# The decoder trunk's up-projections: four more chunks by seven products, a product moved behind the next chunk's first one, and work moved from VectorE to GpSimd

## The chip, the cores and the metric

One Trainium2 chip, one core of it. The core has five engines, each with an instruction queue of its own: TensorE (PE; its weight loads are listed as PEld), VectorE (DVE), ScalarE (ACT), GpSimd (POOL) and SyncE (SP), which here only starts DMAs. Results of TensorE land in PSUM, everything else lies in SBUF. The metric is the device time of one launch in microseconds, the median of several runs; less is better.

## The reference

A trunk of two decoder layers over 512 rows (T) of width 1024 (D), in float32. Layer 0 has dilated attention, layer 1 attends with a forget gate to one shared set of keys and values; both end in the gated ConvFFN, which the larger part of the change is about.

```python
def conv_ffn(xn, w_up, cw, cb, w_down):          # w_up (1024, 5632), w_down (2816, 1024)
    a = xn @ w_up
    T = a.shape[1]
    ap = jnp.pad(a, ((0, 0), (CONV_W - 1, 0), (0, 0)))
    a = sum(ap[:, j:j + T] * cw[j] for j in range(CONV_W)) + cb     # causal, depthwise, width 3
    gate, val = jnp.split(a, 2, axis=-1)
    return (jax.nn.gelu(gate, approximate=True) * val) @ w_down

for l in range(DEPTH):                           # 2 layers
    g = norm_gains[l]
    if l < N_A:
        mix = dilated_mixer(rms_norm(h, g[0]), w_qkv_a[l], w_o_a[l], cos, sin)
    else:
        ...                                      # k_sh, v_sh, c_sh once, from h
        mix = fox_mixer(rms_norm(h, g[0]), w_q_b[j], w_o_b[j], k_sh, v_sh, c_sh)
    h = h + rms_norm(mix, g[1])
    f = conv_ffn(rms_norm(h, g[2]), w_up[l], conv_w[l], conv_b[l], w_down[l])
    h = h + rms_norm(f, g[3])
```

## The kernel before

**Order.** The kernel is scheduled by hand: on each engine the instructions stand in the order in which the Python code issues them, and semaphores join the engines. Tiles come from pools of fixed numbers of buffers (`t8`, `t4`, `t2`; `bank` for the eight PSUM banks).

**Precision.** Each operand of a product is split into a high part (a copy rounded to fp32r) and a low part (the difference), and `mm3` (L276) makes of each product three matmuls: high x high, high x low, low x high (L277 to L279). `Weights` (L33) brings the weights in order: `load` starts the DMA, `high` copies the high part on ScalarE (L60), `low` takes the difference on VectorE (L69), or `low_added` lets a DMA of GpSimd's queue add the raw weight to a negated copy (L62, L86).

**The up-projection** (`ffn`, L630). The 2816 gate and 2816 value columns go in 22 chunks `c` of 128 + 128. A plain chunk makes two banks of 128 x 512: 2 banks x 8 steps of 128 rows x 3 = 48 matmuls of 512 columns. A chunk in `SEVEN` is computed in the form of Strassen and Winograd: the weights' chunk is a 2 x 2 block matrix (A11, A12, A21, A22), the inputs as well, and seven products of half size (A11, S2, S3, A12, S1, A22, S4; 4 steps x 3 = 12 matmuls of 256 columns each, `prod`) take the place of eight. VectorE makes the sums of weights in `first_weights` (L698: S2 and S3, and the sums for the second half) and `other_weights` (L719), the sums of results s12 and s17 in `two_sums` (L993, L994), and o4, o3, o2 (L1010, L1018, L1020). The first product of a chunk, A11, is already made in the chunk before (`open_seven`). Ten of the chunks 5 to 18 go so, in pairs with a plain one between.

**Around a chunk.** `taps` adds the three conv taps of the chunk before: one ScalarE instruction (L639) and two on VectorE (L640, L642) for each of two halves. `glu` applies the gelu on ScalarE; `product` (L650) multiplies gate and value into `hc` on VectorE (L657) and stores the previous one, `hD <- hc`, through GpSimd's queue (L655). `prepare(c, part)` (L750) calls `step`, which moves the weights of the next two chunks on by one stage: `first_weights`, `other_weights` and `plain_weights` are generators, and a `yield` ends a stage. The down-projection works in the same manner on pairs of chunks; its weight sums are made in `down_sums` (L590), some of them long before, and stored in DRAM (`dT`).

**Start.** `warm_up(n)` issues n matmuls on zeros; `transpose0` and `split0` bring blocks of x into place, and `qk0(b, pieces)` makes the first query and key products of block b (L1290).

**End of the second attention** (from L1846). The loop over `m` takes heads in pairs and, from (j, i) = (6, 1), begins to split the last output weights for the products `acc` (`po.both`).

Of the kernel before, what the change touches and what calls it, by code (L numbers as in the profile page):

```python
# [9 lines left out]
F32 = mybir.dt.float32  # L10
# [95 lines left out]
def trunk_kernel(ctx, tc, x, norm_gains, w_qkv_a, w_o_a, w_q_b, w_o_b, kv_norm, w_kvf, b_f,  # L106
# [128 lines left out]
    eps_t = cst.tile([128, 1], F32, name="eps_t")  # L235
    dve.memset(eps_t, EPS)
# [3 lines left out]
    dve.memset(zero, 0.0)  # L240
    warm = bank([128, 512], name="warm")
# [6 lines left out]
    W.load(2)  # L248
    load_x(1, 0)
    load_x(2, 0)  # L250
    load_x(3, 0)
# [338 lines left out]
    def down_sums(pairs, place, queue, lag, behind):  # L590
# [3 lines left out]
        for i in range(n + lag + behind):  # L594
# [35 lines left out]
    def ffn(l, bd, cp, nxt, ahead):  # L630
# [19 lines left out]
        def product():  # L650

            if gated:
# [4 lines left out]
                dve.tensor_tensor(hc[c], bb[:, 0, :], bb[:, 1, :], ALU.mult)  # L657
# [40 lines left out]
        def first_weights(c):  # L698
# [4 lines left out]
            a11, a12, a21, a22 = r0[:, 0:512], r0[:, 512:1024], r1[:, 0:512], r1[:, 512:1024]  # L703
            act.copy(w0[:, 0], r0)
            act.activation(w0[:, 1], r0, AF.Copy, scale=-1.0)
            pool.dma_start(w0[:, 1], r0, accum_op=ALU.add)
            dve.tensor_tensor(sa[:, 0:512], a11, a21, ALU.subtract)
            dve.tensor_tensor(sb[:, 0:512], a21, a22, ALU.add)
            dve.tensor_tensor(sa[:, 512:1024], sb[:, 0:512], a11, ALU.subtract)
            act.copy(w1[:, 0], sa)  # L710
            yield
# [7 lines left out]
        def other_weights(c):  # L719

            a22, sb = half_way.pop(c)
            w2, w3 = (t8([128, 2, 1024], F32R, name="w") for _ in range(2))
            act.copy(w2[:, 0], sb)
            act.copy(w3[:, 0, 0:512], a22)
            yield
            dve.tensor_tensor(w2[:, 1], sb, w2[:, 0].bitcast(F32), ALU.subtract)
            dve.tensor_tensor(w3[:, 1, 0:512], a22, w3[:, 0, 0:512].bitcast(F32), ALU.subtract)
# [22 lines left out]
        def prepare(c, part):  # L750
# [5 lines left out]
            if m in SEVEN:  # L756
                if part == 0 and not after:
                    step(1, m)
                if part == (0 if after else 1) or part == (1 if after else 2):
                    step(2, m)  # L760
# [4 lines left out]
            elif part < 2 or m not in SEVEN:  # L765
                step(1, n)

# [206 lines left out]
        for c in range(2, NF):  # L974
            if c == NF - 4:
                pair_load(0)
            if c == NF - 3:
                sums = down_sums([(l, ND - 1), (1, 8 + l)], in_one, pool, 1, 0)
                next(sums)
            if c in SEVEN:  # L980
# [972 lines left out]
```

## Time and profile before

| what | value |
|---|---|
| runs | 1106.81, 1107.63, 1109.08 us |
| median | 1107.63 us |
| profiled execution | 1107.05 us |
| its span in the profile | 1105.0 us |
| granted TensorE clock | 0.999 |
| TensorE busy | 1096.0 us, 99% |
| VectorE busy | 894.8 us, 81% |
| ScalarE busy | 667.4 us, 60% |
| GpSimd busy | 222.7 us, 20% |

Busy times are unions over a whole execution, so they say nothing of single stages. The line of an instruction is that of the code that issued it, so a helper such as `mm3` has all its matmuls under three lines, and the tile's name tells which stage it is: `up` is the up-projection, `acc` the down-projection and the output projections, `qk_ps` the first query and key products. In a row of the timeline the first number is the start, the second the duration. "waits" lists for how long an engine stood idle just before an instruction, and what released it.

### The profile page before, as it was taken

What the parts mean: (1) busy time and instruction counts of PE and PEld (TensorE: products, weight loads), DVE (VectorE), ACT (ScalarE), POOL (GpSimd) and SP (SyncE); (2) the same over time, 40 slices, a digit from 0 to 9 for tenths busy, and PEclk for the clock granted to TensorE, in tenths of its full rate; (3) what the DMA queues carried; (4) which work ended last, traced back from release to release, by engine and by line L of the source; (5) the groups of instructions that cost most, each with busy time, mean ns of one, the idle gap of its engine ahead of it and who ended that gap; (6) DMA issues with size and microseconds to landing.
All of it is one profiled execution on the core that took longest, in us unless ns stands there. A gap on an engine that the chain in (4) does not pass through costs nothing.

```text
span 1105.0 us, 18176 instructions
## 1 busy us (share of the span) xinstructions
PE 1096.0 (99%) x6608; PEld 948.5 (86%) x6608; DVE 894.8 (81%) x1510; ACT 667.4 (60%) x1120; POOL 222.7 (20%) x331
## 2 busy tenths in 40 slices
PE   9999999999999999999999999999999999999997
PEld 7988889899999988888888778789899999988886
DVE  5677778878887799997877877958978887799994
ACT  6654565656556547576565677655656566547572
POOL 4632101111111111000010766501111111111000
PEclk9999999999999999999999999999999999999999
DMA  9589854468788989894872677574468788999872
GB/s 320 109 290 407 335 151 136 112 148 191 180 194 206 278 312 341 284 321 98 210 153 77 209 229 204 160 233 134 106 146 192 176 200 210 265 314 342 292 248 77
DMA packets 185218, 237.33 MB, mean 215 GB/s; under 512 B 11872, under 2 KB 131672, under 8 KB 184616
## 3 DMA queue, kind: packets, MB, share of 16 engines
q1 hardware_dynamic: 167560, 176.61, 49.9%
q0 software_dynamic: 17568, 59.55, 23.2%
q8 instruction: 52, 0.85, 0.3%
q14 instruction: 38, 0.31, 0.1%
HBM read 170.28 MB, written 39.63 MB: 190 GB/s over the span
## 4 chain that ended last, share of the span: by engine, by line
PE 96%; ACT 2%; DVE 1%; issue 0%; DMA 0%; DVEq 0%; SPq 0%; ACTq 0%
PE up L277 13%; PE up L278 13%; PE up L279 13%; PE acc L277 8%; PE acc L278 8%; PE acc L279 8%; PE qk_ps L1290 2%; PE v_ps L277 2%; PE v_ps L278 2%; PE v_ps L279 2%; PE s_ps L1759 1%; PE o_ps L1806 1%; PE q_ps L277 1%; PE first L279 1%; PE first L277 1%; PE first L278 1%
## 5 line engine op out<-in xcount | busy, mean ns | idle before, releaser
L277 PE MATMUL acc<-w 128*128 128x512 f32 (+1 forms) x311 | 120.5, 388 | 0.0
L279 PE MATMUL acc<-w 128*128 128x512 f32 (+1 forms) x311 | 120.4, 387 | 0.0
L60 ACT CAST w<-wraw 128x1024 fp32r<-128x1024 f32 x96 | 99.0, 1049 | 9.6 <-issue 3.8
L278 PE MATMUL acc<-w 128*128 128x512 f32 (+1 forms) x267 | 103.2, 387 | 0.0
L639 ACT ACTIVATE bb<-up,conv 128x512 f32<-128x512 f32 x80 | 60.0, 776 | 67.3 <-DVE up L1020 42.8
L69 DVE TENSOR_TENSOR w<-wraw,w 128x1024 fp32r<-128x1024 f32 x66 | 88.0, 1353 | 12.9 <-ACT w L60 12.5
L278 PE MATMUL up<-xcl,w 128*128 128x512 f32 (+1 forms) x280 | 96.3, 344 | 0.0
L278 PE MATMUL up<-xbl,w 128*128 128x512 f32 (+1 forms) x280 | 96.3, 344 | 0.0
L277 PE MATMUL up<-xbh,w 128*128 128x512 f32 (+1 forms) x280 | 96.3, 344 | 0.0
L277 PE MATMUL up<-xch,w 128*128 128x512 f32 (+1 forms) x280 | 96.3, 344 | 0.0
L279 PE MATMUL up<-xbh,w 128*128 128x512 f32 (+1 forms) x280 | 96.2, 344 | 0.0
L279 PE MATMUL up<-xch,w 128*128 128x512 f32 (+1 forms) x280 | 96.2, 344 | 0.0
L277 PE MATMUL up<-xsh,w 128*128 128x256 f32 x320 | 90.6, 283 | 0.0
L278 PE MATMUL up<-xsl,w 128*128 128x256 f32 x320 | 90.6, 283 | 0.0
L279 PE MATMUL up<-xsh,w 128*128 128x256 f32 x320 | 90.6, 283 | 0.0
L279 PEld LDWEIGHTS acc<-w 128*128 128x128 f32 x311 | 58.4, 188 | 12.0
L277 PEld LDWEIGHTS acc<-w 128*128 128x128 f32 x311 | 58.4, 188 | 11.7
L642 DVE SCALAR_TENSOR_TENSOR bb<-up,conv,bb 128x510 f32<-128x510 f32 x80 | 59.9, 749 | 2.8
L640 DVE SCALAR_TENSOR_TENSOR bb<-up,conv,bb 128x511 f32<-128x511 f32 x80 | 59.4, 743 | 2.6 <-ACT bb L639 2.6
L277 PEld LDWEIGHTS up<-xsh,w 128*128 128x128 f32 x320 | 61.4, 192 | 0.0
L278 PEld LDWEIGHTS up<-xsl,w 128*128 128x128 f32 x320 | 61.4, 192 | 0.0
L279 PEld LDWEIGHTS up<-xsh,w 128*128 128x128 f32 x320 | 61.4, 192 | 0.0
(336 smaller groups left out, 3157.4 us busy)
## 6 DMA issues: line engine op xcount, KB each, us to landing
wraw<-in_w_up_dram SPq DMA_DIRECT2D x88, 512.0 KB
w<-wraw POOLq DMA_DIRECT2D x50, 512.0 KB, 5.9
dT<-dsums SPq DMA_DIRECT2D x24, 512.0 KB
hD<-hc POOLq DMA_DIRECT2D x44, 256.0 KB, 7.8
dact<-hD SPq DMA_DIRECT2D x44, 256.0 KB
wraw<-dT SPq DMA_DIRECT2D x22, 512.0 KB
wraw<-in_w_down_dram SPq DMA_DIRECT2D x22, 512.0 KB
dsums<-in_w_down_dram SPq DMA_DIRECT2D x18, 512.0 KB
```

What stands on the lines that cost most here:

```text
L60: self.nc.scalar.copy(pair[:, 0, s], raw[:, s])
L69: self.nc.vector.tensor_tensor(pair[:, 1, s], raw[:, s], pair[:, 0, s].bitcast(F32), ALU.subtract)
L277: pe.matmul(o, ah, bh, start=first, stop=False, skip_group_check=shared)
L278: pe.matmul(o, ah, bl, start=False, stop=False, skip_group_check=shared)
L279: pe.matmul(o, al, bh, start=False, stop=last, skip_group_check=shared)
L639: act.activation(bb[:, s, :], ps, AF.Identity, bias=cp[:, 3, ch:ch + 1], scale=cp[:, 2, ch:ch + 1])
L640: dve.scalar_tensor_tensor(bb[:, s, 1:], ps[:, :T - 1], cp[:, 1, ch:ch + 1], bb[:, s, 1:], ALU.mult, ALU.add)
L642: dve.scalar_tensor_tensor(bb[:, s, 2:], ps[:, :T - 2], cp[:, 0, ch:ch + 1], bb[:, s, 2:], ALU.mult, ALU.add)
L1290: pe.matmul(o, ax(0, b, kc)[x], w[:, k, :], start=kc == 0 and x == 0 and w is wh, stop=kc == KD - 1 and w is wl)
L1759: pe.matmul(s[i][hh][:, :nn], q[a][rows, qs], k[b][rows, :nn], start=n == 0, stop=n == 2)
L1806: pe.matmul(o[64 * hh:64 * hh + 64, i * 128:(i + 1) * 128], Vt[hd // 8][:, k, (hd % 8) * 64:(hd % 8) * 64 + 64], pT[j, i, hh][:, k, :], st ...
```

## The change

It has seven parts.

1. `SEVEN` holds all of 5 to 18: four more chunks per layer.
2. In a seven-product chunk, A12 is issued behind A11 of the next chunk, not ahead of S1; the sums o4 and o3 follow right behind A22.
3. The gated product (`hc`) is issued on GpSimd.
4. The low part of A22 is made by a negated copy on ScalarE and an accumulating DMA in GpSimd's queue, no longer by VectorE; the stages of `first_weights` and `other_weights` are cut anew, and the calls of `step` are moved between the products.
5. Start: six and three warm-up matmuls, earlier 4 and 5; the zeros are written first; the first weight, then x of blocks 1 and 2, then the second weight are fetched; the first products go block by block through the first piece, with the transposes of the next block between their matmuls.
6. `down_sums` takes a list of queues; the second of two pairs in `down1` is stored through SP's queue.
7. End of the second attention: the sums of `sums_between` start a step earlier, and so do the high and low parts of the last output weights.

```diff
@@ -25,10 +25,10 @@
 
-SEVEN = (5, 6, 8, 9, 11, 12, 14, 15, 17, 18)
+SEVEN = (5, 6, 7, 8, 9, 10, 11, 12, 13, 14, 15, 16, 17, 18)
 ND = NF // 2
-HALVES = (slice(0, 1024),), (slice(0, 512), slice(512, 1024))
-WARM = 4, 5
+WARM = 6, 3
+HALVES = [(slice(0, 1024),), (slice(0, 512), slice(512, 1024))]
 LAST = 3
@@ -232,12 +232,12 @@
 
+    g_rows = t2([8, 128], name="g0_rows")
+
+    zero = t2([128, 512], BF16, name="zero")
+    dve.memset(zero, 0.0)
     eps_t = cst.tile([128, 1], F32, name="eps_t")
     dve.memset(eps_t, EPS)
-    g_rows = t2([8, 128], name="g0_rows")
-
-    zero = t2([128, 512], BF16, name="zero")
-    dve.memset(zero, 0.0)
     warm = bank([128, 512], name="warm")
@@ -245,9 +245,10 @@
     sp.dma_start(g_rows, norm_gains[0, 0].rearrange("(k p) -> k p", p=128))
-    W.load(2)
+    W.load(1)
     load_x(1, 0)
     load_x(2, 0)
+    W.load(2)
     load_x(3, 0)
@@ -610,7 +611,7 @@
                 for q, t in enumerate(live[i]):
-                    queue.dma_start(dT[l][j, :, q * 1024:q * 1024 + 1024], t)
+                    queue[min(i, len(queue) - 1)].dma_start(dT[l][j, :, q * 1024:q * 1024 + 1024], t)
             yield
@@ -654,7 +655,7 @@
                 hc[c] = t2([128, T], name="hc")
-                dve.tensor_tensor(hc[c], bb[:, 0, :], bb[:, 1, :], ALU.mult)
+                pool.tensor_tensor(hc[c], bb[:, 0, :], bb[:, 1, :], ALU.mult)
@@ -701,14 +702,15 @@
             a11, a12, a21, a22 = r0[:, 0:512], r0[:, 512:1024], r1[:, 0:512], r1[:, 512:1024]
+            dve.tensor_tensor(sa[:, 0:512], a11, a21, ALU.subtract)
+            yield
             act.copy(w0[:, 0], r0)
...
             pool.dma_start(w0[:, 1], r0, accum_op=ALU.add)
-            dve.tensor_tensor(sa[:, 0:512], a11, a21, ALU.subtract)
             dve.tensor_tensor(sb[:, 0:512], a21, a22, ALU.add)
+            yield
             dve.tensor_tensor(sa[:, 512:1024], sb[:, 0:512], a11, ALU.subtract)
             act.copy(w1[:, 0], sa)
-            yield
             dve.tensor_tensor(sb[:, 512:1024], a12, sa[:, 512:1024], ALU.subtract)
@@ -720,11 +722,13 @@
             w2, w3 = (t8([128, 2, 1024], F32R, name="w") for _ in range(2))
+            act.copy(w3[:, 0, 0:512], a22)
+            act.activation(w3[:, 1, 0:512], a22, AF.Copy, scale=-1.0)
+            pool.dma_start(w3[:, 1, 0:512], a22, accum_op=ALU.add)
+            yield
             act.copy(w2[:, 0], sb)
-            act.copy(w3[:, 0, 0:512], a22)
             yield
             dve.tensor_tensor(w2[:, 1], sb, w2[:, 0].bitcast(F32), ALU.subtract)
-            dve.tensor_tensor(w3[:, 1, 0:512], a22, w3[:, 0, 0:512].bitcast(F32), ALU.subtract)
             v = [t.rearrange("p s (q k c) -> p s q k c", q=2, k=4) for t in (w2, w3)]
@@ -753,17 +757,16 @@
             after = c not in SEVEN
-            if m in SEVEN:
-                if part == 0 and not after:
-                    step(1, m)
-                if part == (0 if after else 1) or part == (1 if after else 2):
-                    step(2, m)
+            if m in SEVEN and (after or part):
+                step(2, m)
             if n not in SEVEN:
...
                     step(0, n)
-            elif part < 2 or m not in SEVEN:
+            elif part < 2 or after or m not in SEVEN:
                 step(1, n)
+                if after and part == 0:
+                    step(1, n)
...
@@ -991,31 +994,36 @@
                     dve.tensor_tensor(s12, o2, s1, ALU.add)
+                    if c + 2 in SEVEN:
+                        step(1, c + 2)
                     dve.tensor_tensor(s17, o3, s1, ALU.add)
...
                 prod(o3, w["S3"], (*XA, HI), True)
+                if c + 1 in SEVEN:
+                    step(1, c + 1)
+                    step(2, c + 1)
                 product()
...
                     bb = taps(*before, two_sums)
+                prod(o2, w["S1"], (*XA, LO))
+                prod(o3, w["A22"], (*XB, LO))
+                dve.tensor_tensor(o4, o2, s17, ALU.add)
+                dve.tensor_tensor(o3, o3, s12, ALU.add)
                 prepare(c, 0)
                 glu(before[0], bb)
-                prod(o1, w["A12"], x21)
-                prod(o2, w["S1"], (*XA, LO))
-                prod(o3, w["A22"], (*XB, LO))
-                prepare(c, 1)
-                dve.tensor_tensor(o4, o2, s17, ALU.add)
                 if c + 1 in SEVEN:
...
                     up(*begun, range(4))
+                prod(o1, w["A12"], x21)
                 prod(o2, w["S4"], x22)
-                dve.tensor_tensor(o3, o3, s12, ALU.add)
+                prepare(c, 1)
                 prepare(c, 2)
@@ -1255,7 +1263,7 @@
     def transpose0(b, i):
-        n = 2 if (b, i) == (0, 0) else 4
+        n = 4 if i else 2
         for k0 in range(0, 4, n):
@@ -1276,7 +1284,7 @@
 
-    def qk0(b, *pieces):
+    def qk0(b, *pieces, between=None):
         if b not in qk_banks:
@@ -1284,11 +1292,12 @@
             wh, wl = ws[s]
-            for x, w in ((0, wh), (1, wh), (0, wl)):
-                for k in range(2):
-                    kc = 2 * s + k
-                    pe.matmul(o, ax(0, b, kc)[x], w[:, k, :], start=kc == 0 and x == 0 and w is wh,
-                              stop=kc == KD - 1 and w is wl)
+            for x, w, k in ((0, wh, 0), (1, wh, 0), (0, wh, 1), (1, wh, 1), (0, wl, 0), (0, wl, 1)):
+                kc = 2 * s + k
+                if w is wh and x == 0 and k and between is not None:
+                    between()
+                pe.matmul(o, ax(0, b, kc)[x], w[:, k, :], start=kc == 0 and x == 0 and w is wh,
+                          stop=kc == KD - 1 and w is wl)
@@ -1297,17 +1306,20 @@
     W.split(1)
+    qk0(0, 0, between=L(transpose0, 1, 0))
+    split0(1, 0, (0, 1))
     split0(0, 0, (2, 3))
+    qk0(1, 0, between=L(transpose0, 2, 0))
+    split0(2, 0, (0, 1))
     W.split(2)
-    qk0(0, 0)
-    x0(1, 0)
-    qk0(0, 1)
-    x0(2, 0)
-    qk0(1, 0)
+    split0(1, 0, (2, 3))
+    qk0(2, 0)
+    qk0(0, 1, between=L(transpose0, 3, 0))
+    split0(2, 0, (2, 3))
+    split0(3, 0)
+    qk0(1, 1)
     W.split(3)
-    qk0(1, 1)
-    x0(3, 0)
-    qk0(2, 0, 1)
+    qk0(2, 1)
     W.split(4)
...
@@ -1696,7 +1708,7 @@
     del w4
-    down1 = down_sums([(1, j) for j in range(2)], in_two, pool, 1, 1)
+    down1 = down_sums([(1, j) for j in range(2)], in_two, [pool, sp], 1, 1)
     for c in range(4, 8):
@@ -1829,6 +1841,7 @@
         dve.tensor_tensor(a[:, 0:512], a[:, 512:1024], a[:, 0:512], ALU.subtract)
+        yield
         dve.tensor_tensor(a[:, 512:1024], b[:, 0:512], a[:, 512:1024], ALU.subtract)
@@ -1853,7 +1866,7 @@
         g = sums_between(1, j)
-        for i in ((m, 1), (m + 1, 2), (m + 2, 0), (m + 2, 1)):
+        for i in ((m, 1), (m + 1, 1), (m + 1, 2), (m + 2, 0), (m + 2, 1)):
             sums[i] = g
@@ -1888,9 +1901,9 @@
                 po.both(*fill[2 * m + a - FILL])
-            if live and (j, i) >= (6, 2):
+            if live and (j, i) >= (6, 1):
                 W.low()
-            if live and (j, i) >= (6, 1) and W.n_split < wo + 4:
+            if live and (j, i) >= (6, 0) and W.n_split < wo + 4:
                 W.high()
```

How this moves the instructions, at three places. VectorE in a chunk of seven products, first as it was, from the sums s12 and s17 to the gated product (`csum` is s12 and s17, `bb` the taps, `w<-wsum,w` a low part of weight sums, `up<-up,csum` o4, o3 and o2, `w<-wraw,w` the low part of A22, `hc` the gated product):

```order
L993 TENSOR_TENSOR csum<-up,csum 128x256
L994 TENSOR_TENSOR csum<-up,csum 128x256
L640 SCALAR_TENSOR_TENSOR bb<-up,conv,bb 128x511
L642 SCALAR_TENSOR_TENSOR bb<-up,conv,bb 128x510
L714 TENSOR_TENSOR w<-wsum,w 128x1024
L1010 TENSOR_TENSOR up<-up,csum 128x256
L1018 TENSOR_TENSOR up<-up,csum 128x256
L726 TENSOR_TENSOR w<-wsum,w 128x1024
L727 TENSOR_TENSOR w<-wraw,w 128x512
L1020 TENSOR_TENSOR up<-up,csum 128x256
L657 TENSOR_TENSOR hc<-bb 128x512
```

and in the kernel after, from s17 on:

```order
L999 TENSOR_TENSOR csum<-up,csum 128x256
L641 SCALAR_TENSOR_TENSOR bb<-up,conv,bb 128x511
L643 SCALAR_TENSOR_TENSOR bb<-up,conv,bb 128x510
L641 SCALAR_TENSOR_TENSOR bb<-up,conv,bb 128x511
L643 SCALAR_TENSOR_TENSOR bb<-up,conv,bb 128x510
L1014 TENSOR_TENSOR up<-up,csum 128x256
L1015 TENSOR_TENSOR up<-up,csum 128x256
L710 TENSOR_TENSOR wsum<-wraw 128x512
L712 TENSOR_TENSOR wsum<-wsum,wraw 128x512
L714 TENSOR_TENSOR wsum<-wraw,wsum 128x512
L731 TENSOR_TENSOR w<-wsum,w 128x1024
L1028 TENSOR_TENSOR up<-up,csum 128x256
```

The 512-wide low part and the gated product are gone, the weight sums for the second chunk ahead (`wsum`) now stand in each chunk's list, also where that chunk was plain before, one ahead of s17 and three behind o3, and o4 and o3 stand between taps and weight sums.

GpSimd, in the up-projection of layer 0; before, among the seven-product chunks (`w<-wraw` is an accumulating DMA for a low part, `hD<-hc` the store of the gated product):

```order
L655 DMA hD<-hc 128x512
L706 DMA w<-wraw 128x1024
L655 DMA hD<-hc 128x512
L706 DMA w<-wraw 128x1024
L655 DMA hD<-hc 128x512
```

and after:

```order
L709 DMA w<-wraw 128x1024
L727 DMA w<-wraw 128x512
L656 DMA hD<-hc 128x512
L658 TENSOR_TENSOR hc<-bb 128x512
L709 DMA w<-wraw 128x1024
```

In every chunk there is a second accumulating DMA, of half the width, and the gated product itself stands behind the store of the one before.

VectorE near the end of the second attention, where the last blocks of the pair of heads 6 are normalised (`bias<-bias,rl`) and the last output weights' low parts are taken (`w<-wraw,w`); before:

```order
L1777 RECIPROCAL rl<-ls 128x2
L1779 TENSOR_SCALAR bias<-bias,rl 128x384 x2
L69 TENSOR_TENSOR w<-wraw,w 128x1024
L1777 RECIPROCAL rl<-ls 128x2
L1779 TENSOR_SCALAR bias<-bias,rl 128x512 x2
L69 TENSOR_TENSOR w<-wraw,w 128x1024
```

and after, the place to which the first of these low parts goes, ahead of the last queries' low part (`qst`) and of the next scores:

```order
L1789 RECIPROCAL rl<-ls 128x2
L1791 TENSOR_SCALAR bias<-bias,rl 128x256 x2
L69 TENSOR_TENSOR w<-wraw,w 128x1024
L1579 TENSOR_TENSOR qst<-q_ps,qst 128x512
L1779 ISA bias,nm<-s_ps,bias 128x384
L1779 ISA nm 128x1
```

One low part now stands in front of the four score sums, where before there was none until behind them.

More of the change, by code (lines that the diff above doesn't have):

```diff
@@ L240, in trunk_kernel @@
     dve.memset(zero, 0.0)
+    eps_t = cst.tile([128, 1], F32, name="eps_t")
+    dve.memset(eps_t, EPS)
     warm = bank([128, 512], name="warm")
@@ L977, in ffn @@
             if c == NF - 3:
-                sums = down_sums([(l, ND - 1), (1, 8 + l)], in_one, pool, 1, 0)
+                sums = down_sums([(l, ND - 1), (1, 8 + l)], in_one, [pool], 1, 0)
                 next(sums)
@@ L1339, in trunk_kernel @@
     qk_post(0, 3, qk_banks[3])
-    sums = down_sums([(1, 6), (1, 7)], in_two, sp, 1, 3)
+    sums = down_sums([(1, 6), (1, 7)], in_two, [sp], 1, 3)
     next(sums)
@@ L1370, in v_post @@
         dve.tensor_scalar(V[2][:, b, :], o[:, 256:512], scale_of(1, b), None, ALU.mult)
-    down0 = down_sums([(0, j) for j in range(10)], in_one, sp, 1, 1)
+    down0 = down_sums([(0, j) for j in range(10)], in_one, [sp], 1, 1)
     v_proj0([[L(qk_transpose, 0, 0), L(qk_transpose, 0, 1)],
```

2 lines of the change are left out of this document (removed).

## The prediction

> **What bounds the kernel now.** I read the page first (busy shares, then the chain that ended last), then the waits of TensorE, then the up-projections chunk by chunk in the timeline and the windows view.
>
> ```profile
> span 1105.0 us, 18176 instructions
> PE 1096.0 (99%) x6608; PEld 948.5 (86%) x6608; DVE 894.8 (81%) x1510; ACT 667.4 (60%) x1120; POOL 222.7 (20%) x331
> ...
> PE 96%; ACT 2%; DVE 1%; issue 0%; DMA 0%; DVEq 0%; SPq 0%; ACTq 0%
> ```
>
> TensorE is busy for 99% of the span and is 96% of the chain. The waits view (engine and line, what for: total us, times, longest) has three lines for TensorE and no more:
>
> ```profile
> PE warm L245 <- DVE zero L240: 1.2, 1, 1.2
> PE acc L278 <- DVE w L69: 0.8, 1, 0.8
> PE g_ps L267 <- DMA g_rows<-in_norm_gains_dram: 0.5, 1, 0.5
> ```
>
> So time can go only in two ways: fewer or shorter matmuls, or the start and the one wait of 0.8 us in the second attention. The price of a chunk of the up-projection stands in TensorE's timeline: the first matmul of a plain chunk (4), the first one behind it, and the first matmuls of the S2 products of chunks 5 and 6, which both go by seven products.
>
> ```profile
> 224.65 0.39 PE L277 MATMUL up<-xbh,w 128*128 128x512 f32 x1
> ...
> 235.53 0.28 PE L277 MATMUL up<-xbh,w 128*128 128x256 f32 x1
> ...
> 236.97 0.28 PE L277 MATMUL up<-xsh,w 128*128 128x256 f32 x1
> ...
> 247.04 0.28 PE L277 MATMUL up<-xsh,w 128*128 128x256 f32 x1
> ```
>
> A plain chunk is 48 matmuls of 512 columns in 235.53 - 224.65 = 10.88 us, 0.227 each. A chunk of seven products is 84 matmuls of 256 columns in 247.04 - 236.97 = 10.07 us, 0.120 each, or 1.44 us per product of twelve. Between the two, 0.81 us. The windows view gives both stretches and two more (in each row the window, its length, the busy us and count of PE, PEld, DVE, ACT and POOL, then PE's clock, DMA share, GB/s):
>
> ```profile
> 224.65:235.53 10.88, 10.88 (x49) 9.01 (x48) 9.66 (x15) 6.39 (x8) 1.41 (x2) 1.00 0.46 90
> 236.97:247.04 10.07, 10.07 (x86) 10.07 (x85) 5.98 (x9) 7.18 (x10) 2.25 (x3) 1.00 0.73 163
> 278.12:288.07 9.95, 9.95 (x74) 9.46 (x73) 8.14 (x15) 4.88 (x6) 1.42 (x2) 1.00 1.13 279
> 400.00:420.00 20.00, 20.00 (x90) 16.57 (x89) 19.69 (x27) 12.28 (x16) 3.76 (x7) 1.00 0.89 305
> ```
>
> The clock is granted in full (1.00). VectorE (DVE) is the next engine: 6 to 9.7 us of each ten in the chunks, and 19.69 of 20 in the last chunks of a layer, where the down-projection's sums are made as well. Plain chunks stand between pairs of seven-product chunks now, and VectorE makes up there what it falls behind. The change takes these pauses away, so the question is whether VectorE's work for one chunk fits into 10.07 us.
>
> **Seven products in all of 5 to 18.** Four more chunks in each of two layers: 8 x 0.81 = 6.45 us less on TensorE, if it still waits for nothing. Now VectorE's list. These are its rows in a seven-product chunk of the kernel before; I take the distance from start to start, since the records of neighbours overlap.
>
> ```profile
> 276.25 1.22 DVE L726 TENSOR_TENSOR w<-wsum,w 128x1024 fp32r<-128x1024 f32 x1
> 277.39 0.69 DVE L727 TENSOR_TENSOR w<-wraw,w 128x512 fp32r<-128x512 f32 x1
> ...
> 281.55 0.74 DVE L640 SCALAR_TENSOR_TENSOR bb<-up,conv,bb 128x511 f32<-128x511 f32 x1
> ...
> 284.43 0.68 DVE L707 TENSOR_TENSOR wsum<-wraw 128x512 f32<-128x512 f32 x1
> 285.03 0.68 DVE L708 TENSOR_TENSOR wsum<-wraw 128x512 f32<-128x512 f32 x1
> 285.75 0.69 DVE L709 TENSOR_TENSOR wsum<-wsum,wraw 128x512 f32<-128x512 f32 x1
> 286.47 0.69 DVE L712 TENSOR_TENSOR wsum<-wraw,wsum 128x512 f32<-128x512 f32 x1
> 287.08 0.42 DVE L1010 TENSOR_TENSOR up<-up,csum 128x256 f32<-128x256 f32 x1
> 287.54 0.43 DVE L1018 TENSOR_TENSOR up<-up,csum 128x256 f32<-128x256 f32 x1
> 287.88 1.22 DVE L714 TENSOR_TENSOR w<-wsum,w 128x1024 fp32r<-128x1024 f32 x1
> ```
>
> A 1024-wide difference takes 1.14, a 512-wide sum 0.60 or, where it needs the one ahead of it, 0.72, the four conv taps 2.88 (281.55 to 284.43), a 256-wide sum 0.34, or 0.46 between o4 and o3. After the change a steady chunk holds two 1024-wide (2.28), four 256-wide (1.36) and that pair's first (0.46), the taps (2.88), and four 512-wide (0.60 + 0.72 + 0.72 + 0.61): 9.63 us. With the gated product and the low part of A22 left on VectorE, another 0.60 each, it would be 10.83, more than TensorE's 10.07. So the two moves to GpSimd are what the 6.45 us hang on.
>
> Then I laid the new order out by hand from T, the start of S2 of a chunk, with 0.2 us from the end of a product to the sum that reads it. Sum o2 of the chunk before T+0.2, low part of S2/S3 0.55, s12 1.69, first weight sum 2.03; s17 needs S3 and starts at 3.08; taps 3.42, o4 6.31, o3 6.77, weight sums 7.11 to 9.16, the other low part 9.16, next o2 10.30, which is 0.22 into the next chunk. The list closes on itself with no drift. TensorE's closest wait is A12, at T+7.2 in its new place: it needs o4, which ends at 6.74, 0.4 us ahead. S1 (T+2.9, needs s12) and A22 (T+4.3, needs s17) have 0.8 us or more. That A12 now stands behind A11 of the next chunk is what gives o4 this time. I take 0 for all of this, bounded by the case of a late VectorE below.
>
> **What GpSimd gets.** Per chunk one more accumulating DMA (512 columns) and the gated product. GpSimd's queue as it is, and the copy on ScalarE that it follows:
>
> ```profile
> 281.07 1.07 ACT L705 ACTIVATE w<-wraw 128x1024 fp32r<-128x1024 f32 x1
> ...
> 282.43 0.86 POOL L706 DMA_DIRECT2D w<-wraw  x1 [6.21 <-ACT w L705]
> 282.98 0.88 POOL L655 DMA_DIRECT2D hD<-hc  x1
> ```
>
> An issue takes 0.55 and comes 0.29 after the end of ScalarE's copy. Behind the new wait (A22's accumulation waits for its negated copy) stand the store of hc and the next gated product; both are wanted only a chunk later. ScalarE gets a 512-wide negated copy more, some 0.6 of its 7.18 us in ten. The first price that the trace doesn't show is that of the product on GpSimd. The nearest rows:
>
> ```profile
> 189.63 4.63 POOL L674 TENSOR_TENSOR xsum<-xbh,xbl 128x2048 f32<-128x2048 f32 x1 [51.84 <-DVE xbl L347]
> ...
> 188.86 1.29 DVE L347 TENSOR_TENSOR xbl<-xt_ps,xbh 128x512 fp32r<-128x512 f32 x2 [0.88 <-ACT xbh L346]
> 190.29 5.05 DVE L69 TENSOR_TENSOR w<-wraw,w 128x1024 fp32r<-128x1024 f32 x1
> ...
> 208.62 1.22 DVE L69 TENSOR_TENSOR w<-wraw,w 128x1024 fp32r<-128x1024 f32 x1
> ```
>
> 2048 columns take 4.63 us, so 512 take about 1.16 (an estimate, a quarter). The second row says more: the pair of VectorE sums that read PSUM and SBUF runs across GpSimd's start at 0.65 us each, as ever, but the next difference, which reads SBUF twice, lasts 5.05 instead of 1.22 us and ends 1.08 after GpSimd's sum: it stood still until that was over. The Trainium skill has this as a rule (SBUF — State Buffer, Who interferes with whom): a VectorE instruction with two SBUF inputs and a GpSimd instruction that reads SBUF lock each other out for the whole instruction, and one with a single SBUF input doesn't contend. The trace agrees with both halves (5.05 against 1.22, and 0.65 unchanged). It speaks against this change, so its place decides: the product's start on GpSimd is, by the same layout, at T+2.0 to T+2.35 (ScalarE copies the S2/S3 sums when the second weight sum is there (8.6 in the chunk before), then A22 and its negative (1.0, 0.5 and 0.6 us by the 1.07 of the row above), which ends at 10.7 or T+0.65; +0.29, two issues of 0.55, and up to 0.3 of start-up), and VectorE's only sum with two SBUF inputs near it is the first weight sum, at T+2.03. If VectorE is first, GpSimd waits till 2.7 and then runs under s17 and the taps, which read PSUM: free. If GpSimd is first, VectorE's sum waits till 3.2 and s17 follows at 3.8 instead of 3.08. I take 0 here, with a small margin, and keep the other end for a rival.
>
> In the last chunks (19 to 21) the gated products leave a VectorE that is busy 19.69 of 20 us; there they free 0.60 and may block up to 1.16, three times. I take 0; the bound is 0.5 us a layer.
>
> **The end of the second attention.** The wait of 0.8 us, in the chain:
>
> ```profile
> 701.76 1.14 DVE w L69
> ...
> 702.95 0.50 PE acc L278
> ```
>
> The high and low part of the last output weights now come one step earlier, so this difference is queued ahead of other work, and the matmul finds it ready. Gain 0.8, between 0 (the softmax sums behind it come late instead) and 1.0. The pair of down-projection loads that goes from GpSimd's queue to SP's is issued long before use: 0.
>
> **The start.** From the chain:
>
> ```profile
> 4.94 2.13 PE warm L245 x5
> 7.07 2.56 PE qk_ps L1290 x6
> 9.63 0.52 PE xt_ps L1263 x4
> 10.15 1.38 PE qk_ps L1290 x6
> ```
>
> Three warm-up matmuls instead of five behind the transposes take 0.85 us off (2 x 0.43); the two added ahead of them run while the first gains are fetched, which TensorE waits for anyway. The first six products run at 0.43, the next at 0.23: the same matmul at half the pace. What the change adds is block 1's and 2's transposes between the products, which now need x of these blocks sooner; it is sent ahead of the second weight. I take 0.6: at worst -0.3 (x late), at best 2.2 (0.85, 0.1 of the earlier zeros, and all six at full pace, 6 x 0.2). The Trainium skill (TensorE: Matmul & The Clock Gate, Part 1) explains the half pace by a clock that opens after a stretch of steady work; the rows here agree with a change of pace, and by it fewer warm-ups could move the slow stretch into the products, which the lower end covers.
>
> **The sum.** 6.45 + 0.8 + 0.6 = 7.85 us less than the profiled execution's 1107.05 (span 1105.0 and 2 around it): 1099.2. That execution lies 0.58 under the median of the runs, 1107.63, so I say 1099.8.
>
> **The rivals.**
>
> GpSimd's product gets in first. For it: GpSimd's layout leaves only 0 to 0.3 us between the two, and nothing ties the two engines to an order. Against: start-up on GpSimd adds to its side, and a VectorE that is held back shifts the next chunk. Price: 0.8 to 1.15 us of VectorE per chunk; 0.4 is idle time, so from about 0.45 on TensorE waits (for o4 at A12), and the period becomes 10.5 to 10.8 instead of 10.07. Over 28 chunks that is 12 to 20 us against the 7.85: +4 to +12.6, or 1112 to 1120 by the runs. The change as a whole breaks even at a period of 10.35.
>
> VectorE is a little late. A sum that needs its forerunner costs 0.12 more, a port turn 0.1; if 9.63 becomes 10.15 to 10.3, without a lock-out, 28 x 0.08 to 0.23 = 2 to 6.5 us come back: 1102 to 1106.
>
> It doesn't do what it says elsewhere: start or tail lose 1 to 3 us while the chunks gain, 1100 to 1104, or accumulating DMAs, one more per chunk where the DMA share was already 1.13 of 1 with rows that overlap, land late and TensorE stands for A22: anything from 1103 to 1112.
>
> **How the numbers follow.** All covered: 0.58, own range 1097 to 1103 (7.85 with the start between -0.3 and 2.2, attention 0 to 1, tail up to 1). VectorE a little late: 0.13. GpSimd first: 0.22. The rest: 0.07. A measurement of this kernel tells 0.2%, 2.2 us, from no change. Faster by more: 0.58, 0.10 of the second, 0.04 of the rest, 0.72. The same: 0.04. Slower: 0.22 and 0.02, 0.24. The range goes from 1097 up to 1112, the lower edge of the GpSimd case; the rest of that case, about 0.2, stays outside.
>
> **What would show it.** Right: TensorE's waits have no new line in the up-projections, S2 to S2 of neighbouring chunks takes 10.07 in all of 5 to 18, the gated product on GpSimd (about 1.2 us) starts after the first weight sum of its chunk, which still lasts 0.68. Wrong: that weight sum lasts 1.5 or more, TensorE waits for o4 at A12 or for s17 at A22 in chunk after chunk, and S2 to S2 is 10.4 or more; or a line "PE acc <- DVE w" is still there in the second attention; or the first six products at the start stand no earlier in the chain than 7.07.

## The result, and the profile after

The changed kernel takes 1118.58 us (median of 4 runs, 1118.32 to 1119.88), the kernel before beside it 1107.31: a ratio of 1.0102 (95% interval 1.0088 to 1.0116). It is 1.0% slower, where 0.7% faster was forecast. The profiled execution took 1119.88 us, 1.3 over the median, with a span of 1117.9. Its page, in the same parts as before (busy time of the first engines, the chain by engine), and TensorE's waits:

```profile
span 1117.9 us, 19013 instructions
PE 1097.8 (98%) x6896; PEld 958.0 (86%) x6896; DVE 953.0 (85%) x1534; ACT 691.2 (62%) x1164; POOL 301.2 (27%) x393
...
PE 67%; DVE 20%; issue 7%; DMA 2%; ACT 2%; POOL 1%; SPq 0%; DVEq 0%; POOLq 0%; ACTq 0%
```

```profile
PE up L278 <- DVE csum L999: 7.5, 19, 0.4
PE xt_ps L1271 <- DMA h<-in_x_dram: 1.5, 1, 1.5
PE warm L245 <- DVE eps_t L240: 1.2, 1, 1.2
PE o_ps L1818 <- ACT pT L1805: 0.9, 2, 0.6
```

VectorE now holds 20% of the chain (1% before), and TensorE waits for s17 (L999) in the up-projections. The waits of its weight loads (PEld) show a second sum that comes late, o4 (L1014):

```profile
PEld up L278 <- DVE csum L999: 12.0, 21, 0.6
PEld up L278 <- DVE up L1014: 6.1, 21, 0.3
```

The matmuls' own waits add up to 7.5 us only: a record of a matmul is 0.28 us long where the next one starts after 0.12, so the records cover a part of each gap. The chunks' own distance tells more. The sum o2 ends a chunk; here are its first and last of each layer (chunks 5 and 18), before and after, from VectorE's timeline:

```profile
247.25 0.43 DVE L1020 TENSOR_TENSOR up<-up,csum 128x256 f32<-128x256 f32 x1 [0.26 <-PE up L279]
382.95 0.43 DVE L1020 TENSOR_TENSOR up<-up,csum 128x256 f32<-128x256 f32 x1 [2.12 <-PE up L279]
828.27 0.43 DVE L1020 TENSOR_TENSOR up<-up,csum 128x256 f32<-128x256 f32 x1 [0.26 <-PE up L279]
963.97 0.43 DVE L1020 TENSOR_TENSOR up<-up,csum 128x256 f32<-128x256 f32 x1 [2.12 <-PE up L279]
```

```profile
246.88 0.43 DVE L1028 TENSOR_TENSOR up<-up,csum 128x256 f32<-128x256 f32 x1 [0.24 <-PE up L280]
389.94 0.43 DVE L1028 TENSOR_TENSOR up<-up,csum 128x256 f32<-128x256 f32 x1 [1.54 <-PE up L280]
834.91 0.43 DVE L1028 TENSOR_TENSOR up<-up,csum 128x256 f32<-128x256 f32 x1 [0.24 <-PE up L280]
976.75 0.43 DVE L1028 TENSOR_TENSOR up<-up,csum 128x256 f32<-128x256 f32 x1 [1.54 <-PE up L280]
```

| stretch | before | after | difference |
|---|---|---|---|
| start to o2 of chunk 5, layer 0 | 247.25 | 246.88 | -0.4 |
| chunks 5 to 18, layer 0 | 135.70 | 143.06 | +7.4 |
| to chunk 5 of layer 1 (down-projection, second attention) | 445.32 | 444.97 | -0.4 |
| chunks 5 to 18, layer 1 | 135.70 | 141.84 | +6.1 |
| to the end of the span | 141.03 | 141.15 | +0.1 |

The chunks lose 13.5 us, a little more than the 12.9 by which the span grew. One chunk on VectorE and on GpSimd:

```profile
278.46 0.69 DVE L714 TENSOR_TENSOR wsum<-wraw,wsum 128x512 f32<-128x512 f32 x1
279.07 1.22 DVE L731 TENSOR_TENSOR w<-wsum,w 128x1024 fp32r<-128x1024 f32 x1
280.20 0.42 DVE L1028 TENSOR_TENSOR up<-up,csum 128x256 f32<-128x256 f32 x1
280.54 1.21 DVE L716 TENSOR_TENSOR w<-wsum,w 128x1024 fp32r<-128x1024 f32 x1
281.67 0.42 DVE L996 TENSOR_TENSOR csum<-up,csum 128x256 f32<-128x256 f32 x1
282.00 2.15 DVE L705 TENSOR_TENSOR wsum<-wraw 128x512 f32<-128x512 f32 x1
284.08 0.41 DVE L999 TENSOR_TENSOR csum<-up,csum 128x256 f32<-128x256 f32 x1
...
291.27 0.43 DVE L1028 TENSOR_TENSOR up<-up,csum 128x256 f32<-128x256 f32 x1
```

```profile
280.85 0.86 POOL L727 DMA_DIRECT2D w<-wraw  x1 [5.60 <-ACT w L726]
281.39 0.88 POOL L656 DMA_DIRECT2D hD<-hc  x1
281.98 1.62 POOL L658 TENSOR_TENSOR hc<-bb 128x512 f32<-128x512 f32 x1
```

The first weight sum (L705), an instruction of 0.68 us, lasts 2.15 and ends at 284.15, 0.55 after GpSimd's gated product (281.98 + 1.62 = 283.60): it did its whole work when that was over. I call this standing still a hold. From o2 to o2 it is 291.27 - 280.20 = 11.07 us, and VectorE has no pause in it: its list of 9.63 and the 1.45 for which it stood. On TensorE the first two matmuls of A22 come 0.67 and 0.22 us after the one ahead of them (at 284.54 and 284.76, behind s17), and the first two of A12 0.37 and 0.22 (at 287.77 and 287.99, behind o4), where 0.12 is usual: 0.65 and 0.35 us, together the 1.00 by which 11.07 exceeds 10.07. The line of that sum over the kernel (count, busy us, mean ns):

```profile
L705 DVE TENSOR_TENSOR wsum<-wraw 128x512 f32<-128x512 f32 x28 | 50.4, 1798 | 0.0
```

(1.798 - 0.68) x 28 = 31 us of standing still, which is 21 of the 28 sums at about 1.47. Six of the other seven are the first three of each layer. The seventh stands between held ones in layer 1, in a chunk in which GpSimd's issues came late:

```profile
914.35 0.68 DVE L705 TENSOR_TENSOR wsum<-wraw 128x512 f32<-128x512 f32 x1
```

```profile
915.10 1.62 POOL L658 TENSOR_TENSOR hc<-bb 128x512 f32<-128x512 f32 x1
```

With the sum 0.75 us ahead of the product nothing was held, and o2 followed o2 in 9.75 us; the next sum, at 924.10, was held again (2.23). This one chunk accounts for the difference between the 7.4 us that layer 0 lost and the 6.1 of layer 1.

### The profile page after: what moved, and what is told of

Same layout as the page of the kernel before. It is cut to its first block, busy times and chain, and to the rows that moved or that the text cites. A ratio compares the mean times of both kernels' runs of the same rounds, so it can differ in the third digit from the quotient of the medians.

```text
span 1117.9 us, 19013 instructions
## 1 busy us (share of the span) xinstructions
PE 1097.8 (98%) x6896; PEld 958.0 (86%) x6896; DVE 953.0 (85%) x1534; ACT 691.2 (62%) x1164; POOL 301.2 (27%) x393
## 4 chain that ended last, share of the span: by engine, by line
PE 67%; DVE 20%; issue 7%; DMA 2%; ACT 2%; POOL 1%; SPq 0%; DVEq 0%; POOLq 0%; ACTq 0%
PE acc L278 8%; PE acc L280 8%; PE acc L279 8%; PE up L278 6%; PE up L279 6%; PE up L280 6%; DVE wsum L705 4%; DVE bb L643 3%; DVE bb L641 3%; PE qk_ps L1299 2%; PE o_ps L1818 2%; DVE w L716 2%; PE pT_ps L1803 2%; PE first L280 1%; PE first L278 1%
## 5 line engine op out<-in xcount | busy, mean ns | idle before, releaser
L278 PE MATMUL up<-xsh,w 128*128 128x256 f32 x448 | 128.9, 288 | 7.8 <-DVE csum L999 7.5
L279 PE MATMUL up<-xsl,w 128*128 128x256 f32 x448 | 126.7, 283 | 0.0
L280 PE MATMUL up<-xsh,w 128*128 128x256 f32 x448 | 126.6, 283 | 0.0
L278 PEld LDWEIGHTS up<-xsh,w 128*128 128x128 f32 x448 | 85.8, 191 | 12.0 <-DVE csum L999 12.0
L278 PE MATMUL up<-xbh,w 128*128 128x256 f32 (+1 forms) x264 | 86.0, 326 | 1.0
L278 PE MATMUL up<-xch,w 128*128 128x256 f32 (+1 forms) x264 | 85.9, 325 | 0.9
L279 PEld LDWEIGHTS up<-xsl,w 128*128 128x128 f32 x448 | 85.8, 192 | 0.0
L280 PEld LDWEIGHTS up<-xsh,w 128*128 128x128 f32 x448 | 85.8, 192 | 0.0
L279 PE MATMUL up<-xbl,w 128*128 128x256 f32 (+1 forms) x264 | 84.9, 321 | 0.0
L279 PE MATMUL up<-xcl,w 128*128 128x256 f32 (+1 forms) x264 | 84.9, 321 | 0.0
L280 PE MATMUL up<-xch,w 128*128 128x256 f32 (+1 forms) x264 | 84.8, 321 | 0.0
L280 PE MATMUL up<-xbh,w 128*128 128x256 f32 (+1 forms) x264 | 84.8, 321 | 0.0
L658 POOL TENSOR_TENSOR hc<-bb 128x512 f32<-128x512 f32 x44 | 68.3, 1552 | 26.6 <-ACT bb L661 26.5
L727 POOL DMA_DIRECT2D w<-wraw x28 | 24.0, 858 | 151.5 <-ACT w L726 145.1
```

Source lines behind the costliest of these rows:

```text
L278: pe.matmul(o, ah, bh, start=first, stop=False, skip_group_check=shared)
L279: pe.matmul(o, ah, bl, start=False, stop=False, skip_group_check=shared)
L280: pe.matmul(o, al, bh, start=False, stop=last, skip_group_check=shared)
L658: pool.tensor_tensor(hc[c], bb[:, 0, :], bb[:, 1, :], ALU.mult)
L727: pool.dma_start(w3[:, 1, 0:512], a22, accum_op=ALU.add)
```

## The experiments

The theory going in was the first rival of the prediction: GpSimd's product and VectorE's sum lock each other out, and GpSimd is first. The rival to this was that some other part (the recut stages, A12's place, A22's low part by a DMA) costs the time. Each kernel is the one after with the edit shown, if nothing else is said; each ratio is to the kernel before, run beside it.

**1. The gated product back on VectorE.**

```diff
-                pool.tensor_tensor(hc[c], bb[:, 0, :], bb[:, 1, :], ALU.mult)
+                dve.tensor_tensor(hc[c], bb[:, 0, :], bb[:, 1, :], ALU.mult)
```

> Theory (lock-out): in the kernel after, GpSimd's gated product starts 0.02 us ahead of VectorE's first weight sum and holds it up by 1.45 us in each chunk, so VectorE's list of 9.63 us becomes 11.08. With the product back on VectorE nothing is held up and the list is 9.63 + 0.60 = 10.23 us: chunk to chunk 10.2 to 10.3 us, the first weight sum 0.68 us, 1103 us (1101.5 to 1104.5). Rival (the recut stages, A12's place, or A22's low part by DMA cost the time): still 1116 us or more.

Measured: 1100.93 us, ratio 0.9947 (0.9933 to 0.9962). That is below the kernel before, with this one word undone. The chunk, in VectorE's timeline:

```profile
287.06 0.42 DVE L1028 TENSOR_TENSOR up<-up,csum 128x256 f32<-128x256 f32 x1
...
289.46 0.68 DVE L705 TENSOR_TENSOR wsum<-wraw 128x512 f32<-128x512 f32 x1
...
297.26 0.42 DVE L1028 TENSOR_TENSOR up<-up,csum 128x256 f32<-128x256 f32 x1
```

10.20 us per chunk against 10.23 from the list, the sum at 0.68. The other parts of the change don't cost the time; the rival falls.

**2. The first weight sum ahead of s12**, so that VectorE comes 0.34 us earlier.

```diff
-                    dve.tensor_tensor(s12, o2, s1, ALU.add)
                     if c + 2 in SEVEN:
                         step(1, c + 2)
+                    dve.tensor_tensor(s12, o2, s1, ALU.add)
```

> The first weight sum is issued ahead of s12, 0.34 us earlier on VectorE; nothing else changes. Theory: VectorE now comes about 0.3 us before GpSimd, the weight sum lasts 0.68 us, the gated product runs behind it under sums that read PSUM, chunk to chunk 10.07 to 10.12 us, 1100.5 us (1099 to 1102). Rival: the work on GpSimd costs as such, in whatever order: 1116 us or more.

Measured: 1138.26 us, 1.0280 (1.0263 to 1.0297). A miss by 38 us, to the other side:

```profile
295.24 1.21 DVE L716 TENSOR_TENSOR w<-wsum,w 128x1024 fp32r<-128x1024 f32 x1
296.38 2.55 DVE L705 TENSOR_TENSOR wsum<-wraw 128x512 f32<-128x512 f32 x1
```

```profile
295.64 0.86 POOL L727 DMA_DIRECT2D w<-wraw  x1 [6.55 <-ACT w L726]
296.18 0.88 POOL L656 DMA_DIRECT2D hD<-hc  x1
296.76 1.61 POOL L658 TENSOR_TENSOR hc<-bb 128x512 f32<-128x512 f32 x1
```

The sum's record starts 0.38 us ahead of the product's, and still it ends 0.56 after it (298.93 against 298.37). So the start of a GpSimd record isn't the moment that counts. The product is handed over while the issue of the store (L656) goes on, till 297.06; from there to 298.37 it is 1.31 us, the length that it has elsewhere alone. I took it that GpSimd claims what the two engines share (the port, below) at that hand-over, and VectorE, which had it till the end of its low part (296.45), lost it there.

**3. The product half a chunk later**, behind the accumulating DMA of the next weights.

```diff
-                product()
...
                 prepare(c, 0)
+                product()
                 glu(before[0], bb)
```

> The gated product is issued half a chunk later, behind the accumulating DMA of the next weights, so that it falls under the conv taps and o4, which read PSUM. Theory: product 1.3 us long, no instruction of VectorE stretched, chunk to chunk 10.07 to 10.12 us, 1100.5 us (1099 to 1102). Rival: 1116 us or more.

Measured: 1118.01 us, 1.0099 (1.0084 to 1.0114). Also a miss: the first weight sum is 0.68 again, but the product met the next one (L710). I had read its place from the held-up schedule; without the hold, the taps come 1.4 us earlier against ScalarE's copies.

```profile
296.64 1.62 POOL L658 TENSOR_TENSOR hc<-bb 128x512 f32<-128x512 f32 x1
```

```profile
296.71 2.11 DVE L710 TENSOR_TENSOR wsum<-wraw 128x512 f32<-128x512 f32 x1
```

Again 0.56 from the product's end to the sum's (298.26, 298.82). It is the meeting, not this sum.

**4. Zeros instead of the product**, in the same place (the gated product is left out).

```diff
-                pool.tensor_tensor(hc[c], bb[:, 0, :], bb[:, 1, :], ALU.mult)
+                pool.memset(hc[c], 0.0)
```

> In place of the gated product GpSimd fills hc with zeros (the product is left out): same place and same tile, but it reads nothing. Theory, as far as it is GpSimd's reading that locks: no stretched weight sum, chunk to chunk 10.07 to 10.12 us, 1100.5 us (1099 to 1102). If GpSimd's writing locks VectorE too: weight sum stretched to about 1 us, 1103 to 1110 us. Rival: 1116 us or more.

Measured: 1098.66 us, 0.9924 (0.9909 to 0.9939), chunk to chunk 10.08. The two meet as before, and nothing is held:

```profile
297.90 0.85 POOL L656 DMA_DIRECT2D hD<-hc  x1
298.47 0.83 POOL L658 MEMSET hc<- 128x512 f32 x1
```

```profile
298.45 0.68 DVE L705 TENSOR_TENSOR wsum<-wraw 128x512 f32<-128x512 f32 x1
```

Neither the issues nor writing hold VectorE; what is left is what GpSimd reads. And 1098.66, with the product gone, is the mark for the change when its product holds nothing.

**5. The old ten chunks**, all else as changed: `SEVEN = (5, 6, 8, 9, 11, 12, 14, 15, 17, 18)`.

> The kernel after with the old ten chunks by seven products; everything else as changed. Theory (lock-out makes VectorE the bound only where seven-product chunks follow each other without a pause): the plain chunk in each three gives VectorE back what the held-up sums take, the chunks take 31.1 us in threes as before, and what is left is the gain of the start and the attention, 0.9 us each: 1105.3 us (1104 to 1107.5). Rival (the product on GpSimd costs TensorE time wherever it stands): 1110 us or more.

Measured: 1117.70 us, 1.0101 (1.0086 to 1.0116). A miss: I expected the plain chunks to give the time back. TensorE's longest entry and a held sum:

```profile
PE up L278 <- DVE csum L996: 9.9, 7, 2.2
```

```profile
317.38 2.43 DVE L710 TENSOR_TENSOR wsum<-wraw 128x512 f32<-128x512 f32 x1
```

Two causes are possible: the hold, or the new order, in which S1 follows S3 at once and wants s12 earlier behind a plain chunk. Run 9 divides them.

**6. The first weight sum ahead of the low part of S2/S3**, so that VectorE is in a 1.2 us instruction when GpSimd is given its product.

```diff
                     dve.tensor_tensor(s12, o2, s1, ALU.add)
-                    if c + 2 in SEVEN:
-                        step(1, c + 2)
...
+                if c + 2 in SEVEN:
+                    step(1, c + 2)
                 if c + 1 in SEVEN:
                     step(1, c + 1)
                     step(2, c + 1)
```

> The first weight sum is issued ahead of the low part of S2/S3, 1.5 us earlier; VectorE then has o2, weight sum, low part, s12, s17. Theory, refined by the second run: GpSimd claims the port as soon as its product is handed to it, behind the store's issue, up to 0.6 us ahead of its record, and whichever instruction of VectorE is due next stands until the product's end. Here the low part (1.2 us) has started 0.9 us ahead of that record, so it is through when GpSimd gets its turn, and the product falls under s12, s17 and the taps: no stretched instruction, chunk to chunk 10.07 to 10.1 us, 1099 us (1098 to 1101). If GpSimd's claim is earlier than 0.9 us: the low part stretched to about 3.6 us, chunk to chunk over 12 us, 1138 us or more. If it isn't the place but the product as such: 1116 us or more.

Measured: 1100.08 us, 0.9937 (0.9922 to 0.9952), chunk to chunk 10.11.

```profile
287.88 0.68 DVE L705 TENSOR_TENSOR wsum<-wraw 128x512 f32<-128x512 f32 x1
288.47 1.22 DVE L716 TENSOR_TENSOR w<-wsum,w 128x1024 fp32r<-128x1024 f32 x1
```

```profile
288.81 0.89 POOL L656 DMA_DIRECT2D hD<-hc  x1
289.40 1.63 POOL L658 TENSOR_TENSOR hc<-bb 128x512 f32<-128x512 f32 x1
```

The low part starts 0.93 ahead of the product's record and runs through it unstretched; a sum that started 0.38 ahead (run 2) did not. The claim lies between, and the store's issue in front of the product starts 0.58 to 0.59 ahead. The sum of the changed kernel that escaped (at 914.35) started 0.75 ahead, which narrows it further.

**7. The order of run 2, and more work on GpSimd**: zeros are written into hc ahead of the product.

```diff
+                pool.memset(hc[c], 0.0)
                 pool.tensor_tensor(hc[c], bb[:, 0, :], bb[:, 1, :], ALU.mult)
```

> The order of the second run (first weight sum ahead of s12), and a write of zeros into hc ahead of the gated product on GpSimd, which only adds work there (0.5 to 0.8 us). Theory: the extra work moves GpSimd's claim behind the start of the weight sum, which lasts 0.68 us again instead of 2.55; more work on GpSimd makes the kernel faster by 38 us: 1099.5 us (1098 to 1101.5). Rival (work on GpSimd costs as such): 1138 us or more.

Measured: 1098.72 us, 0.9928 (0.9911 to 0.9944). A useless instruction per chunk takes 39.5 us off run 2:

```profile
297.66 0.68 DVE L706 TENSOR_TENSOR wsum<-wraw 128x512 f32<-128x512 f32 x1
```

```profile
298.02 0.86 POOL L658 MEMSET hc<- 128x512 f32 x1
298.96 1.30 POOL L659 TENSOR_TENSOR hc<-bb 128x512 f32<-128x512 f32 x1
```

The product now falls under sums and taps that read PSUM, and costs nothing. Only at the first of these chunks of each layer is a sum still held (1.51 and 1.44 us), without a wait of TensorE. The kernel's time is that of run 4, where there is no product at all (1098.66).

**8. The kernel before, with all of 5 to 18 by seven products** and nothing else.

> The kernel before with all of chunks 5 to 18 by seven products and nothing else. Theory: VectorE's list is 9.63 + 0.60 + 0.60 = 10.83 us per chunk, so chunk to chunk 10.8 to 11.1 us and 28 x 0.45 to 0.75 = 13 to 21 us more: 1120 us (1116 to 1128). Rival (VectorE has room, the two moves to GpSimd weren't needed): 1101 us.

Measured: 1180.26 us, 1.0661 (1.0645 to 1.0677), far more than expected. A chunk takes 13.6 us; the window of one (busy us of PE, PEld, DVE, ACT, POOL, then PE's clock) and TensorE's wait:

```profile
302.10:315.70 13.60, 11.82 (x86) 11.62 (x86) 10.92 (x18) 6.64 (x9) 1.41 (x2) 0.88 0.57 136
```

```profile
PE up L277 <- DVE up L1010: 39.7, 24, 1.8
```

VectorE's 10.92 are close to the 10.83 of the list, so the list alone doesn't make 13.6. On TensorE, 1.9 of the 3.5 us over 10.07 are waiting for o4 (L1010), which stands behind the next chunk's weight sums there: the matmul that needs it (at 312.50) starts 2.06 after the one ahead of it, not 0.12. The other 1.6 are slower matmuls behind that stop, 0.21 from one to the next, at a clock that is 0.88 over the chunk. VectorE then waits for TensorE in turn. This kernel lacks the new order as well as the two moves to GpSimd, so it doesn't show what the moves alone are worth; that the sums right behind A22 and the recut stages are needed where such chunks follow each other is my reading of o4's place, and was not tried by itself.

**9. The old ten chunks and the gated product on VectorE**, the edits of runs 5 and 1 together.

> The old ten chunks, as in the fifth run, and the gated product back on VectorE; it asks why that run lost 11 us, where the lock-out theory gave 1105.3. If the lock-out held VectorE there too (weight sums of 2.4 us were seen): nothing is stretched and 1105.3 us (1104 to 1107.5) come out now. If it is the new order (S1 stands right behind S3, so behind a plain chunk s12 is wanted 1.44 us earlier than with A12 between, while VectorE has two taps ahead of it): TensorE still waits for s12 up to 2.2 us in each pair, 1114 us or more. I lean to the second, with a part for the first: 1112 us.

Measured: 1108.15 us, 1.0007 (0.9997 to 1.0016), and TensorE's waits for s12:

```profile
PE up L278 <- DVE csum L996: 1.8, 4, 0.6
```

Of the loss of run 5, 9.5 us were the hold and the rest, some 3 us against the 1105.3, is left with the product on VectorE and with waits for s12. I had leaned the other way. How these 3 us divide between the order and VectorE's longer list wasn't tried.

**10. The order of run 2, with the store in two issues.**

```diff
-                    pool.dma_start(hD[c - 1], hc.pop(c - 1))
+                    t = hc.pop(c - 1)
+                    for s in (slice(0, 256), slice(256, 512)):
+                        pool.dma_start(hD[c - 1][:, s], t[:, s])
```

> The first weight sum ahead of s12, and the store of hc in two issues of half the width ahead of the gated product in place of the write of zeros. Theory as refined (GpSimd claims the port when its product is handed over, while the issue ahead of it still goes): the second issue of 0.55 us moves the claim behind the start of the weight sum, no stretched instruction, chunk to chunk 10.1 us, 1099.5 us (1098 to 1101.5). If the claim comes with the first of the two issues already: weight sum stretched to 3 us, 1140 us or more.

Measured: 1099.70 us, 0.9934 (0.9919 to 0.9949), chunk to chunk 10.11, the sum 0.68 to 0.69 (held only at the first of these chunks of each layer, 1.40 and 1.36). The claim comes with the last issue ahead of the product, not the first. In the last chunks of this run a 1024-wide difference that started 0.60 us ahead of the product (at 408.22) was held, 3.00 us instead of 1.22, and one 0.81 ahead (at 976.97) was not: with the sum at 914.35 that puts the claim 0.60 to 0.75 us ahead of the record. Runs 6, 7 and 10 keep everything of the change and beat both kernels; run 6 does it without an added instruction, run 10 with one issue more per chunk.

## Why the prediction was wrong, point by point

**Which way.** Wrong: 1099.8 was forecast, 1118.6 came. It is the first rival (0.22), with its mechanism, its place (the first weight sum, then s17, and TensorE at A12 for o4; the wait for s17 at A22, which came with it, it named only among the signs) and its range of 1112 to 1120. That the range held is in part luck: the period was longer than the rival's 10.5 to 10.8, but 21 chunks were held, not 28: 21 x 1.00 - 7.85 = +13.1 us.

**The step that failed** is the race: "the product's start on GpSimd is ... at T+2.0 to T+2.35", VectorE's sum at T+2.03, so I took 0, where it cost TensorE 1.00 us in each of 21 chunks. Two things were wrong in it. The start-up of up to 0.3 us, which I put on GpSimd's side, isn't there (the product's record starts 0.59 after that of the store's issue, which takes 0.55), and what counts is earlier still: 0.60 to 0.75 us ahead of the record, about when the store's issue starts. Then the two aren't independent, though I wrote that nothing ties them to an order. Both follow the same weight sum, L712, which ends at 278.42:

```profile
278.45 1.05 ACT L713 CAST w<-wsum 128x1024 fp32r<-128x1024 f32 x1 [0.50 <-DVE wsum L712]
```

From 278.46 on VectorE has L714, L731, o2, L716 and s12 to do, 3.54 us (to 282.00), and ScalarE's three copies, of which this is the first, and GpSimd's two issues take 3.52 (to 281.98). A VectorE that is held back does shift the next chunk, as I had counted against the rival, but GpSimd shifts with it, so the meeting comes back in every chunk, and it came back at once after the one chunk that escaped. The 0.4 us of idle time softened it as the rival says: 1.45 of standing, less the 0.44 between 9.63 and 10.07, is the 1.0 by which the period grew.

**The page that spoke against the change** was right where it mattered. The Trainium skill (SBUF — State Buffer, Who interferes with whom) says that only GpSimd's reads meet VectorE's second SBUF input, and that whoever issues first holds the pair for the whole instruction. Runs 3 and 4 agree with the first half (2.11 us with a product, 0.68 with zeros). For the second, run 2 shows that "first" can't be read from the records: a sum with a start 0.38 us ahead stood for the whole product.

**The price of a hold** was 0.8 to 1.15; it is 1.47: the product takes 1.30 alone, not 1.16, and VectorE starts only behind it. Hence 11.07 per chunk, not 10.5 to 10.8. A quarter of 4.63 leaves out what doesn't grow with the width; the kernel before has a smaller row too:

```profile
26.61 0.46 POOL L1097 TENSOR_TENSOR tu<-qk,rope 128x128 f32<-128x128 f32 x1 [0.64 <-ACT qk L1091]
```

A straight line through 0.46 for 128 columns and 4.63 for 2048 gives 1.29 for 512 (an estimate).

**TensorE's saving** of 0.81 per chunk was right: run 4 has 10.08 per chunk, run 7 10.11. **VectorE's list** was right: 10.20 against 10.23 in run 1, and 9.63 + 1.45 = 11.08 after. That "the 6.45 us hang on" both moves was too strong: with the gated product back on VectorE, run 1 lost 0.13 per chunk and 2.3 us in all against run 4. What the move of A22's low part is worth was not tried by itself.

**A12, S1, A22 and the new DMA.** No wait for A22's low part shows in any run, so it lands in time. The 0.4 us that o4 had ahead of A12 and the 0.8 that s17 had ahead of A22 did not survive the hold: in a held chunk TensorE loses 0.35 us at A12 and 0.65 at A22.

**The second attention.** The wait for the low part (0.8 us) is gone, as forecast; two waits for `pT`, 0.9 us together, are new. The stretch gained 0.4 us after, and with run 7 0.7 (444.57 between its o2 sums of chunks 18 and 5, against 445.32); over all runs with this part it is 0.1 to 0.9, one profile each.

**The start.** 0.6 was forecast, 0.4 came, with a new wait of 1.5 us for x of block 1. That landing varies: run 2 waits 1.8, run 7 0.2, and run 7 reaches chunk 5 1.6 us earlier than the kernel before.

**The tail.** VectorE was held there too (a 1024-wide difference at 409.11 took 2.41 us instead of 1.22), with next to no effect on TensorE: +0.1 us.

## What to carry to other kernels

Before moving an elementwise product from VectorE to GpSimd, list VectorE's instructions that read SBUF twice near its new place, and put the product where a stretch of VectorE's work reads PSUM; it cost nothing there in run 7, and its whole length where the two met. If both engines' turns follow from the same earlier instruction, a meeting isn't chance that averages out, but can repeat in every round, as here in 21 chunks. A margin of a few tenths between two engines, laid out by hand, is no ground for taking the cost as 0.

## What was not expected of the hardware

GpSimd's claim on the shared port comes 0.60 to 0.75 us ahead of the product's record when a DMA issue stands right in front of it (run 10 and the chunk at 914.35 after the change; runs 2 and 6 agree). With a write of zeros in front it doesn't: in run 7, in the first chunks, two differences with both inputs in SBUF stand on VectorE one behind the other (x2), 2.36 us for both, so neither was held, and the second started about 0.25 us ahead of the product's record. It was the product that waited there (2.12 us instead of 1.30). Why the two cases differ was not tried.

```profile
210.06 2.36 DVE L688 TENSOR_TENSOR xsl<-xsum,xsh 128x1024 fp32r<-128x1024 f32 x2 [1.47 <-ACT xsh L687]
```

```profile
211.45 2.12 POOL L659 TENSOR_TENSOR hc<-bb 128x512 f32<-128x512 f32 x1
```

The granted clock fell to 0.88 in the chunks of run 8, in which TensorE stops for 1.8 us in every 13.6: it was 0.57 in the 4 us behind a stop (312.4 to 316.4) and 1.00 ahead of it (303 to 312). The length of the stop alone doesn't explain it: in run 2 TensorE stops for 1.7 us in every 11.96, and the clock stays at 1.00. What makes the difference was not tried.
